# A hybrid attention and RWKV-7 layer: lead-in by halves of the sequence, bias vectors stored from another queue, and priority for the first substitution

## The chip, the cores and the metric

The kernel runs on one core of one Trainium2 chip. The metric is device microseconds of one execution, lower is better. TensorE is called PE (its weight loads PEld), VectorE DVE, ScalarE ACT, GpSimd POOL, and the queue that issues most DMAs SP. ACT issues some DMAs as well.

## What is computed

One decoder layer over 512 tokens and 16 learned meta tokens, with 1024 channels and 16 heads of 64. Attention with a sliding window and RWKV-7 time mixing run side by side on the same projections:

```
h = layer_norm(concat(meta, x), ln0_g, ln0_b)            # 528 x 1024
proj = h @ w_in                                          # q, k, v, RWKV columns, two gates
att = sliding-window attention(q, k, v) with rel_bias[t5_bucket(distance)] and sinks
z = token_shift(RWKV columns, shift_mu)                  # r, k, v, wl, al, gl
decay = exp(-exp(-softplus(-(w0 + tanh(wl) @ w2)) - 0.5)); a = sigmoid(a0 + al @ a2)
S = S * decay + (S @ -kk) (kk a)^T + v k^T ; y = S r     # a recurrence over tokens, per head
rw = (group_norm(y) + bonus) * (sigmoid(gl) @ g2)
merged = sigmoid(gate_att) * att + sigmoid(gate_rwkv) * rw
h = layer_norm(ALPHA * h + merged @ w_out); h = layer_norm(ALPHA * h + relu(h @ w_ff1)**2 @ w_ff2)
```

All arithmetic is float32. A product with a weight matrix is made of three matmuls over rounded high and low parts (hi x hi, hi x lo, lo x hi).

## The kernel before

**Lead-in.** Four tiles xt0 to xt3 of 128 tokens each and the meta tokens xm are loaded and normalised (normalize, L229: statistics on DVE, the inverse root on POOL, the scaling on ACT or DVE). PE then turns each of the eight column tiles (transpose, L303), ACT or DVE scales and shifts it into hfull (L306, L308), ACT rounds it into hhi (L311), and DVE makes the residual hlo (L312). These two, 1024 channels by 528 tokens, are the moving operand of every projection.

**Dense units.** A unit (dense, L366) multiplies one 128-column tile of w_in with all tokens, in two spans of 264 tokens, each 8 x 3 matmuls (L331 to L333) into one of two PSUM banks of the pool dn. After each span evict takes the bank out: ACT scales it (L412), and DVE adds the shifted neighbour (mix, L406). The weights come through load (L263): a DMA into one of two tiles wraw, a rounding on ACT (whi, L258) and a residual on DVE (wlo, L261), with three buffers each. The first units are wa (decay and learning-rate inputs), gl (gate input), k0, r0, ak, v0: the keys, reads and values of the first head pair and the attention keys.

**Scan.** For each of eight head pairs, rwkv_lora (L481) turns wa's rows zw and za into the decay and the rate (tw and ta, L491), rwkv_keys and rwkv_reads build the operands AX and BK, rwkv_scores the score blocks, and rwkv_inverse (L746) inverts 16 x 16 diagonal blocks by substitution: 30 small DVE operations on Xf and ftmp, a copy into Xr, two stores to DRAM. rwkv_inverse_place (L775) loads them back as X and XB, and rwkv_blocks (L791) of the next stage multiplies with X on PE (up, L811).

**Attention bias.** One matmul (tbp, L985) gives the bias by distance for 16 heads, a copy puts it into tbs, and a DMA (L989) stores it 128 times into tbd in DRAM. aside_query loads a slanted view of it (bias, L1056). aside_gate_rwkv loads the gate's matrix gw (L1096) and rounds it on ACT (gwh, L1097).

**What sets the order.** PE's order is written by hand: weave (L379) steps through the dense units and calls other work at the times of a table. The other engines' orders come from a scheduler that takes instructions by priority; the context manager ahead(n) raises it by n. Each engine then runs its own list strictly in that order, and so do the DMA issues of SP and of ACT: an instruction that waits holds all behind it. Buffers go round within a pool by tag, and a tile waits for the readers of the one that had its place.

Of the kernel before, what the change touches and what calls it, by code (L numbers as in the profile page):

```python
# [20 lines left out]
P = 128  # L21
# [110 lines left out]
def hybrid_layer_kernel(ctx: ExitStack, tc: tile.TileContext, I: dict, out: bass.AP):  # L132
# [39 lines left out]
    xt = [xp.tile([P, D], F32, name=f"xt{b}", tag=f"xt{b}") for b in range(4)]  # L172
    xm = xp.tile([NMETA, D], F32, name="xm")
    rows = xp.tile([NCOLS, P], F32, name="rows")
    for b in range(4):
        nc.sync.dma_start(xt[b], I["x"][b * P : (b + 1) * P, :])
    nc.scalar.dma_start(xm, I["meta"])
    nc.scalar.dma_start(rows, I["rows"][0:NCOLS])
    a0, w0 = CONSTS["ident"]
    nc.scalar.dma_start(con[:, a0 : a0 + w0], I["consts"][:, a0 : a0 + w0])  # L180
# [14 lines left out]

    vps = pg.tile([P, 512], F32, name="vps", tag="g")
    pe.transpose(vps[:, :NCOLS], rows, ident[:NCOLS, :NCOLS])
    vc = cst.tile([P, NCOLS], F32, name="vc")
    act.copy(vc, vps[:, :NCOLS])
# [48 lines left out]
    moments0 = [normalize(xt[b], P, str(b), b < 2) for b in range(4)]  # L248
    normalize(xm, NMETA, "m", False)
# [25 lines left out]
    early = {COL_WA: load("w_in", COL_WA // P)}  # L275

    hhi = hpool.tile([P, KT, T], F32R, name="hhi")
    hlo = hpool.tile([P, KT, T], F32R, name="hlo")
    tm = pch.tile([P, 512], F32, name="tm", tag="Y", bufs=PS[3])
    for k in range(KT):  # L280
        pe.transpose(
            tm[:, k * NMETA : (k + 1) * NMETA], xm[:, k * P : (k + 1) * P], ident[:NMETA, :NMETA]
        )
    fm = xp.tile([P, KT, NMETA], F32, name="fm")
    m = slice(0, NMETA)

# [6 lines left out]
    dve.tensor_tensor(fm, fm, cols("ln0_b"), op=ALU.add)
    act.copy(hhi[:, :, m], fm)
    dve.tensor_tensor(hlo[:, :, m], fm, hhi[:, :, m].bitcast(F32), op=ALU.subtract)
    for k in range(KT):
        ks = slice(k * P, (k + 1) * P)
        if k % 2 == 0:
            tp = pg.tile([P, 512], F32, name="tp", tag="g")
        else:  # L300
            tp = pat.tile([P, 512], F32, name="tp", tag="a")
        for b in range(4):
            pe.transpose(tp[:, b * P : (b + 1) * P], xt[b][:, ks], ident)  # L303
        full = xp.tile([P, SEQ], F32, name="hfull", tag="hfull", bufs=4)
        if k % 2 == 0:
            act.activation(full, tp, AF.Identity, bias=vcol("ln0_b", k), scale=vcol("ln0_g", k))  # L306
        else:
            dve.tensor_scalar(  # L308
                full, tp, vcol("ln0_g", k), vcol("ln0_b", k), op0=ALU.mult, op1=ALU.add
            )  # L310
        act.copy(hhi[:, k, NMETA:], full)  # L311
        dve.tensor_tensor(  # L312
            hlo[:, k, NMETA:], full, hhi[:, k, NMETA:].bitcast(F32), op=ALU.subtract
        )

# [83 lines left out]
    def shifted(col, mrow, tag, after, spans=ALLT):  # L399
# [8 lines left out]
        def evict(ps, t0, n):  # L408
            if t0 == spans[0][0]:
                s["z"] = ew.tile([P, T], F32, name=tag, tag=tag)  # L410
                s["edge"] = ew.tile([P, 1], F32, name="edge", tag="edge", bufs=2)
            act.activation(s["z"][:, t0 : t0 + n], ps[:, :n], AF.Copy, scale=dcol("omu", mrow))  # L412
# [336 lines left out]
    def rwkv_inverse(j):  # L749
# [11 lines left out]
        for s in range(B - 1):  # L761
            nj, nt = s + 1, B - 1 - s
            tv = tmp[:, 0 : nj * nt].rearrange("p (j t) -> p j t", j=nj)
            dve.tensor_tensor(  # L764
                tv, Xf[:, 0:nj, s : s + 1].to_broadcast([NB, nj, nt]),
                Nf[:, s : s + 1, s + 1 :].to_broadcast([NB, nj, nt]), op=ALU.mult,
            )
            dve.tensor_tensor(Xf[:, 0:nj, s + 1 :], Xf[:, 0:nj, s + 1 :], tv, op=ALU.add)  # L768
        dve.tensor_copy(Xr, Xf[0:64].rearrange("p a b -> p b a"))
# [219 lines left out]
    nc.sync.dma_start(tbd, tbs.unsqueeze(1).to_broadcast([HEADS, P, P]))  # L989
# [335 lines left out]
    marks = [6]  # L1325
# [91 lines left out]
    with tc.manual_schedule(engines={mybir.EngineType.PE}):  # L1417
        for s in range(-1, PAIRS + 1):
# [257 lines left out]
```

## Time and profile before

| what | us |
|---|---|
| three runs | 995.95, 1003.83, 999.57 |
| their median | 999.57 |
| the profiled execution | 997.59 |
| its span | 995.8 |
| PE busy in the span | 946.2 |
| DVE busy | 654.3 |
| ACT busy | 469.6 |

The profile is of one further execution. Its span is the time from the first to the last instruction; 1.8 us lie around it. A row of the timeline gives the start, the duration, the engine, the line, and the tile written and those read; a bracket gives the engine's idle time just before and what ended it. A busy PE is not PE at its peak: the clock that the throttle granted (PEclk) is listed apart, 1.00 being full.

### The profile page before, as it was taken

Reading aid. Unit: us, or ns where it says so; the run is one execution under the profiler, and the core shown is the slowest. Engines: PE = TensorE matmul, PEld = TensorE weight load, DVE = VectorE, ACT = ScalarE, POOL = GpSimd, SP = SyncE. Lnnn points to the kernel's source line nnn. Section 1 sums busy time; section 2 is a strip of 40 time slices with the busy share of each in tenths; the row PEclk is TensorE's granted clock in tenths of the full one; section 3 lists DMA queues with packets and bytes.
Section 4 is the critical chain, followed back from the end, with each engine's and each line's share of the span. In section 5 each row is a group of like instructions: output and inputs, shape, how many; then the busy total and the mean of one; then the engine's idle time right before and its main releaser. Section 6 shows DMA issues by size and latency. Waiting matters only on the chain.

```text
span 995.8 us, 19206 instructions
## 1 busy us (share of the span) xinstructions
PE 946.2 (95%) x7533; PEld 790.8 (79%) x7533; DVE 654.3 (66%) x1503; ACT 469.6 (47%) x1238; POOL 43.4 (4%) x108
## 2 busy tenths in 40 slices
PE   4999899999999999999998999899999999999996
PEld 3988788888888887878886677788888888888885
DVE  8577688787887878778867865766433234543437
ACT  6535448465584575745736822843422124442220
POOL 2000000010010000100001000100000000000001
PEclk9999899999999999999999999899999999999999
DMA  7544332433224432233444535133232323323232
GB/s 269 94 126 125 99 81 67 126 76 104 76 50 124 104 112 68 70 109 88 129 124 104 171 106 212 64 106 127 86 106 74 117 86 104 95 95 100 71 105 84
DMA packets 82674, 105.47 MB, mean 106 GB/s; under 512 B 47766, under 2 KB 54664, under 8 KB 82584
## 3 DMA queue, kind: packets, MB, share of 16 engines
q1 hardware_dynamic: 81088, 102.16, 35.1%
q10 hardware_dynamic: 1496, 2.08, 0.6%
q8 instruction: 59, 0.97, 0.4%
q14 instruction: 31, 0.25, 0.1%
HBM read 86.29 MB, written 13.74 MB: 100 GB/s over the span
## 4 chain that ended last, share of the span: by engine, by line
PE 69%; DVE 17%; ACT 8%; issue 2%; DMA 2%; SPq 0%; POOL 0%; DVEq 0%; ACTq 0%; POOLq 0%
PE dps L331 12%; PE dps L332 11%; PE dps L333 11%; PE acc L1486 6%; PE acc L1488 6%; PE acc L1487 6%; DVE wlo L261 2%; ACT Z L744 2%; PE sc L659 2%; PE o L1273 2%; PE av L1180 2%; DVE AX L884 2%; PE o L1275 1%; PE o L1274 1%; DVE Xf L768 1%
## 5 line engine op out<-in xcount | busy, mean ns | idle before, releaser
L261 DVE TENSOR_TENSOR wlo<-wraw,whi 128x512 fp32r<-128x512 f32 x242 | 159.4, 685 | 175.3 <-ACT whi L258 174.9
L258 ACT CAST whi<-wraw 128x512 fp32r<-128x512 f32 x242 | 141.8, 618 | 274.3 <-PE dps L332 135.2
L331 PE MATMUL dps<-hhi,whi 128*128 128x264 f32 (+1 forms) x640 | 219.1, 342 | 3.4 <-DVE ftmp L764 1.4
L332 PE MATMUL dps<-hlo,whi 128*128 128x264 f32 (+1 forms) x640 | 204.9, 320 | 1.4 <-DVE hlo L312 1.4
L333 PE MATMUL dps<-hhi,wlo 128*128 128x264 f32 (+1 forms) x640 | 204.1, 319 | 0.4 <-DVE wlo L261 0.4
L331 PEld LDWEIGHTS dps<-hhi,whi 128*128 128x128 f32 x640 | 121.8, 190 | 17.1 <-issue 3.0
L333 PEld LDWEIGHTS dps<-hhi,wlo 128*128 128x128 f32 x640 | 121.4, 190 | 9.1 <-DVE wlo L261 0.6
L332 PEld LDWEIGHTS dps<-hlo,whi 128*128 128x128 f32 x640 | 121.8, 190 | 6.9 <-DVE hlo L312 2.5
L331 PE MATMUL dps<-h1hi,whi 128*128 128x512 f32 (+1 forms) x264 | 100.1, 380 | 3.8 <-ACT h1f L1536 3.8
L332 PE MATMUL dps<-h1lo,whi 128*128 128x512 f32 (+1 forms) x264 | 100.3, 380 | 0.0
L333 PE MATMUL dps<-h1hi,wlo 128*128 128x512 f32 (+1 forms) x264 | 99.9, 379 | 0.0
L331 PEld LDWEIGHTS dps<-h1hi,whi 128*128 128x128 f32 x264 | 50.4, 191 | 12.9 <-ACT h1f L1536 4.1
L332 PEld LDWEIGHTS dps<-h1lo,whi 128*128 128x128 f32 x264 | 50.4, 191 | 9.3 <-DVE h1lo L1542 0.2
L333 PEld LDWEIGHTS dps<-h1hi,wlo 128*128 128x128 f32 x264 | 50.4, 191 | 9.1
L1486 PE MATMUL acc<-whi,hhi 128*128 128x512 f32 x128 | 50.7, 396 | 0.0
L1488 PE MATMUL acc<-whi,hlo 128*128 128x512 f32 x128 | 50.4, 394 | 0.0
L1487 PE MATMUL acc<-wlo,hhi 128*128 128x512 f32 x128 | 50.0, 391 | 0.0
L1486 PE MATMUL acc<-whi,fhi 128*128 128x512 f32 x112 | 43.6, 389 | 0.0
L1487 PE MATMUL acc<-wlo,fhi 128*128 128x512 f32 x112 | 43.6, 389 | 0.0
L1488 PE MATMUL acc<-whi,flo 128*128 128x512 f32 x112 | 43.6, 389 | 0.0
L897 ACT ACTIVATE Z<-ch,PC 64x64 f32<-64x64 f32 x56 | 17.3, 308 | 45.6 <-DVE Z L895 44.3
L744 ACT COPY Z<-vt 64x64 f32<-64x64 f32 x128 | 26.4, 206 | 9.0 <-PE vt L737 7.6
(292 smaller groups left out, 1721.9 us busy)
## 6 DMA issues: line engine op xcount, KB each, us to landing
wraw<-in_w_ff_dram SPq DMA_DIRECT2D x64, 512.0 KB, 3.6
wraw<-in_w_in_dram SPq DMA_DIRECT2D x52, 512.0 KB, 4.1
wraw<-in_w_out_dram SPq DMA_DIRECT2D x8, 512.0 KB, 3.8
xt<-in_x_dram SPq DMA_DIRECT2D x4, 512.0 KB
Nd<-NT SPq DMA_DIRECT2D x16, 128.0 KB, 3.0
bv<-bv SPq DMA_DIRECT2D x8, 256.0 KB
bvm<-bv SPq DMA_DIRECT2D x8, 256.0 KB, 3.4
qs<-qhi SPq DMA_DIRECT2D x16, 128.0 KB, 4.0
```

Source lines behind the costliest of these rows:

```text
L258: act.copy(hi[:n, qs], raw[:n, qs])
L261: dve.tensor_tensor(lo[:n, qs], raw[:n, qs], hi[:n, qs].bitcast(F32), op=ALU.subtract)
L331: pe.matmul(ps, whi, xhi, start=first, stop=False)
L332: pe.matmul(ps, whi, xlo, start=False, stop=False)
L333: pe.matmul(ps, wlo, xhi, start=False, stop=last)
L659: pe.matmul(scs[e][:, c * P : (c + 1) * P], BK[ER[e], 4 * i + c, :], AXg[ER[e], e, 4 * i + c], start=True, stop=True,)
L744: act.copy(Z[2 * i + cc][64 * (1 - e) : 64 * (1 - e) + 64, e, :], vt[64 * cc : 64 * cc + 64, i * P + e * HD : i * P + (e + 1) * HD],)
L884: dve.tensor_tensor(AXg[:, e, cs], AXg[:, e, cs], gqs[e].rearrange("p (c k t) -> p c k t", c=4, k=2), op=ALU.add,)
L1180: pe.matmul(av[64 * e : 64 * e + 64, (2 * i + n) * P : (2 * i + n + 1) * P], vs[:, 2 * i + n], ps[:, 2 * n + e, :], start=(d == 0), stop=( ...
L1486: pe.matmul(acc[b], xhi[k][:, bs], hi[:, ws], start=first, stop=False)
L1487: pe.matmul(acc[b], xhi[k][:, bs], lo[:, ws], start=False, stop=False)
L1488: pe.matmul(acc[b], xlo[k][:, bs], hi[:, ws], start=False, stop=last)
```

## The change

It has three parts.

First, the lead-in. The order of the first loads changes: the identity, blocks 0 and 1 of x, the first weights, blocks 2 and 3; the parameter rows and the meta tokens by ACT's queue. Blocks 2 and 3 use a buffer of AX. Tokens are turned in halves of 256: tokens(0, k) makes four pairs of column tiles of the first half ahead of the first dense unit, and second_tokens(k) the second half, at times 3.6 to 4.2 of the first stage. The generator spans_first runs the first spans of wa, gl and k0 in turn, then their second spans. The low-rank steps move from 9.0 and 10.4 to 16.8 and 17.6.

Second, the bias by distance becomes distance_bias, called at 7.0. Its copy tbs takes the buffer of gw, and the store into tbd is issued by ACT.

Third, the substitution of the first pair gets the priority PRI["up"].

```diff
-    xt = [xp.tile([P, D], F32, name=f"xt{b}", tag=f"xt{b}") for b in range(4)]
+    xt = [xp.tile([P, D], F32, name=f"xt{b}", tag=f"xt{b}") for b in range(2)]
+    xt23 = rw.tile([P, 2, D], F32, name="xt23", tag="AX", bufs=NBUF["AX"])
+    xt += [xt23[:, d] for d in range(2)]
...
+    nc.scalar.dma_start(rows, I["rows"][0:NCOLS])
+    nc.scalar.dma_start(xm, I["meta"])
+    nc.sync.dma_start(con[:, a0 : a0 + w0], I["consts"][:, a0 : a0 + w0])
+    wfirst = wst.tile([P, D], F32, name="wraw", tag="wraw", bufs=WB[2])
     for b in range(4):
+        if b == 2:
+            nc.sync.dma_start(wfirst, I["w_in"][COL_WA // P])
         nc.sync.dma_start(xt[b], I["x"][b * P : (b + 1) * P, :])
...
-    moments0 = [normalize(xt[b], P, str(b), b < 2) for b in range(4)]
-    normalize(xm, NMETA, "m", False)
+    with ahead(500):
+        normalize(xm, NMETA, "m", True)
+        moments0 = [normalize(xt[b], P, str(b), b == 0) for b in range(2)]
...
+    def tokens(u, k):
+        pool_, tag = ((pg, "g"), (pat, "a"))[k // 2 % 2]
+        tp = pool_.tile([P, 512], F32, name="tp", tag=tag)
+        t4 = tp.rearrange("p (d t) -> p d t", d=2)
+        if u == 0:
+            full = xp.tile([P, 2, 2 * P], F32, name="hfull", tag="hfull", bufs=4)
         else:
+            full = rw.tile([P, 2, 2 * P], F32, name="hfull", tag="NT", bufs=NBUF["NT"])
+        for d in range(2):
+            for b in range(2):
+                pe.transpose(
+                    t4[:, d, b * P : (b + 1) * P],
+                    xt[2 * u + b][:, (k + d) * P : (k + d + 1) * P], ident,
+                )
+        for d in range(2):
+            g_, b_ = vcol("ln0_g", k + d), vcol("ln0_b", k + d)
+            if d == 0:
+                act.activation(full[:, d], t4[:, d], AF.Identity, bias=b_, scale=g_)
+            else:
+                dve.tensor_scalar(full[:, d], t4[:, d], g_, b_, op0=ALU.mult, op1=ALU.add)
+        ts_ = slice(NMETA + u * 2 * P, NMETA + (u + 1) * 2 * P)
+        act.copy(hhi[:, k : k + 2, ts_], full)
         dve.tensor_tensor(
+            hlo[:, k : k + 2, ts_], full, hhi[:, k : k + 2, ts_].bitcast(F32), op=ALU.subtract
         )
...
+    with ahead(450):
+        meta_tokens()
+        for k in range(0, KT, 2):
+            tokens(0, k)
+        early = {COL_WA: split(wfirst)}
+    with ahead(450):
+        moments0 += [normalize(xt[b], P, str(b), b == 2) for b in range(2, 4)]
...
-        for s in range(B - 1):
...
+        with ahead(PRI["up"] if j == 0 else 0):
+            for s in range(B - 1):
...
-    tbp = dn.tile([P, 512], F32, name="tbp", tag="dn")
-    pe.matmul(tbp[0:HEADS, 0:P], relb, cv("onehot")[0:NBUCKETS], start=True, stop=True)
-    tbs = at.tile([P, 2 * P], F32, name="tbs", tag="bias", bufs=2)[0:HEADS, 0:P]
-    act.copy(tbs, tbp[0:HEADS, 0:P])
     tbd = dr.tile([HEADS, P, P], F32, name="tbd")
-    nc.sync.dma_start(tbd, tbs.unsqueeze(1).to_broadcast([HEADS, P, P]))
+    def distance_bias():
+        tbp = pat.tile([P, 512], F32, name="tbp", tag="a")
+        pe.matmul(tbp[0:HEADS, 0:P], relb, cv("onehot")[0:NBUCKETS], start=True, stop=True)
+        tbs = at.tile([P, P], F32, name="tbs", tag="gw")[0:HEADS]
+        act.copy(tbs, tbp[0:HEADS, 0:P])
+        nc.scalar.dma_start(tbd, tbs.unsqueeze(1).to_broadcast([HEADS, P, P]))
...
-    unit("wa", COL_WA, shifted(COL_WA, 24, "k", low_rank))
-    unit("gl", COL_GL, shifted(COL_GL, 25, "r", gate_rank))
-    keys(0)
+    def spans_first(first, *then):
+        for gen in (first, *then):
+            for _ in range(KT):
+                yield next(gen)
+        yield from first
+    order += [COL_WA, COL_GL]
+    gl = shifted(COL_GL, 25, "r", gate_rank)
+    k0 = shifted(COL_K, 8, "k", partial(rwkv_keys, 0))
+    units.append(("wa", spans_first(shifted(COL_WA, 24, "v", low_rank), gl, k0)))
+    units.append(("gl", gl))
+    unit("k0", COL_K, k0)
...
-                    (9.0, ("wa",), F(rwkv_lora, 0, 0)),
-                    (10.4, (), F(rwkv_lora, 0, 1)),
-                    (20.0, ("k0",), F(rwkv_sums, 0)),
+                    (16.8, ("wa",), F(rwkv_lora, 0, 0)),
+                    (17.6, (), F(rwkv_lora, 0, 1)),
+                    (24.0, ("k0",), F(rwkv_sums, 0)),
+                    (7.0, (), distance_bias),
+                ] + [(3.6 + 0.2 * k, (), F(second_tokens, k)) for k in range(0, KT, 2)] + [
```

What the change makes of the engines' lists is seen at three places. After the first units' weights the orders of PE, SP, ACT and DVE differ in places up to the end of the first pair's substitution, and from there on in names alone.

On SP, after the constants, before (lw: a low-rank weight, kd: the attention keys):

```order
L427 DMA con<-in_consts_dram 128x1602
L474 DMA lw<-in_lora_dram 128x256
L268 DMA wraw<-in_w_in_dram 128x1024 x2
L1096 DMA gw<-in_gate_w_dram 128x128
L989 DMA tbd<-tbs 2048x1x128
L268 DMA wraw<-in_w_in_dram 128x1024 x2
```

and now, at the same place:

```order
L454 DMA con<-in_consts_dram 128x1602
L501 DMA lw<-in_lora_dram 128x256
L276 DMA wraw<-in_w_in_dram 128x1024 x2
L501 DMA lw<-in_lora_dram 128x256
L1087 DMA bias<-tbd 128x2x128
L1127 DMA gw<-in_gate_w_dram 128x128
L1087 DMA bias<-tbd 128x2x128
L276 DMA wraw<-in_w_in_dram 128x1024
```

The store has left SP, and two loads of its result now stand on both sides of gw's load, ahead of the fourth weight tile of the queue. The first of them waits for the store's end.

On ACT, from the copy of the bias to the low-rank step, before:

```order
L987 COPY tbs<-tbp 16x128
L412 ACTIVATE k<-dps,drv 128x264
L414 COPY edge<-dps 128x1
L1097 CAST gwh<-gw 128x128
L258 CAST whi<-wraw 128x512
L412 ACTIVATE k<-dps,drv 128x264
L258 CAST whi<-wraw 128x512
L438 ACTIVATE twl<-k 64x528
```

and now (v, r, k are the three first units' outputs):

```order
L1019 COPY tbs<-tbp 16x128
L1020 DMA tbd<-tbs 2048x1x128
...
L469 CAST za<-tal 64x528
L1128 CAST gwh<-gw 128x128
L266 CAST whi<-wraw 128x512
L439 ACTIVATE r<-dps,drv 128x264
L266 CAST whi<-wraw 128x512
L474 ACTIVATE sg<-r 128x512
L518 ACTIVATE tw<-dps,drv 128x264 x2
```

The store follows its copy at once, and gwh has moved behind zw and za, but ahead of two weight casts, of gl's second eviction and of the first low-rank evictions tw.

On SP, at the end of the first pair's substitution, before:

```order
L771 DMA xtd_270<-Xf 66x16x16
L1069 DMA qs_1318<-qhi 64x512
L1069 DMA qs_1318<-qlo 64x512
L1069 DMA qs_1319<-qhi 64x512
L1069 DMA qs_1319<-qlo 64x512
L772 DMA Xr_954<-Xr 64x256
L783 DMA XB<-xtd_270 64x8x64 x2
L781 DMA X_1173<-Xr_954 128x8x16
```

and now:

```order
L800 DMA xtd_240<-Xf 66x16x16
L801 DMA Xr_964<-Xr 64x256
L1100 DMA qs_1328<-qhi 64x512
L1100 DMA qs_1329<-qhi 64x512
L1100 DMA qs_1328<-qlo 64x512
L1100 DMA qs_1329<-qlo 64x512
L810 DMA X_1183<-Xr_964 128x8x16
L812 DMA XB<-xtd_240 64x8x64 x2
```

Xr's store has moved ahead of the four stores of the queries, and X's load ahead of XB's but still behind those four.

On DVE, the same end, before:

```order
L764 TENSOR_TENSOR ftmp<-Xf,Nf 66x15
L583 TENSOR_TENSOR AX<-r,Px 64x8x64
L768 TENSOR_TENSOR Xf<-Xf,ftmp 66x15
L583 TENSOR_TENSOR AX<-r,Px 64x8x64
L769 COPY Xr<-Xf 64x256
L1060 SCALAR_TENSOR_TENSOR qlo<-dps,qhi 128x512
```

and now:

```order
L793 TENSOR_TENSOR ftmp<-Xf,Nf 66x15
L568 SCALAR_TENSOR_TENSOR BK<-u,drv,iP 64x8x64
L797 TENSOR_TENSOR Xf<-Xf,ftmp 66x15
L574 SCALAR_TENSOR_TENSOR BKm<-u,drv,iP 64x16
L798 COPY Xr<-Xf 64x256
L568 SCALAR_TENSOR_TENSOR BK<-u,drv,iP 64x8x64
L574 SCALAR_TENSOR_TENSOR BKm<-u,drv,iP 64x16
L610 TENSOR_TENSOR AX<-r,Px 64x8x64
L612 SCALAR_TENSOR_TENSOR rk<-r,vc,kp 128x512
L1091 SCALAR_TENSOR_TENSOR qlo<-dps,qhi 128x512
```

One BK, one BKm and one AX have moved from ahead of Xr's copy to behind it, and rk from behind qlo to ahead of it.

More of the change, by code (lines that the diff above doesn't have):

```diff
@@ L246, in normalize @@
         return mv[:, 0:1], r
[L248 to L249 removed]
+    with ahead(500):
+        normalize(xm, NMETA, "m", True)
+        moments0 = [normalize(xt[b], P, str(b), b == 0) for b in range(2)]
+    vps = pg.tile([P, 512], F32, name="vps", tag="g")
+    pe.transpose(vps[:, :NCOLS], rows, ident[:NCOLS, :NCOLS])
+    vc = cst.tile([P, NCOLS], F32, name="vc")
+    act.copy(vc, vps[:, :NCOLS])
     def split(raw, hi=None, lo=None, n=P):
@@ L293, in hybrid_layer_kernel, with meta_tokens @@
[L293 to L299, printed above, removed]
-        else:
[L301 to L311, printed above, removed]
+    def meta_tokens():
+        tm = pch.tile([P, 512], F32, name="tm", tag="Y", bufs=PS[3])
+        for k in range(KT):
+            pe.transpose(
+                tm[:, k * NMETA : (k + 1) * NMETA], xm[:, k * P : (k + 1) * P], ident[:NMETA, :NMETA]
+            )
+        fm = xp.tile([P, KT, NMETA], F32, name="fm")
+        m = slice(0, NMETA)
+        dve.tensor_tensor(
+            fm, tm[:, 0:P].rearrange("p (k t) -> p k t", k=KT), cols("ln0_g"), op=ALU.mult
+        )
+        dve.tensor_tensor(fm, fm, cols("ln0_b"), op=ALU.add)
+        act.copy(hhi[:, :, m], fm)
+        dve.tensor_tensor(hlo[:, :, m], fm, hhi[:, :, m].bitcast(F32), op=ALU.subtract)
@@ L312, in hybrid_layer_kernel, with second_tokens @@
         dve.tensor_tensor(
-            hlo[:, k, NMETA:], full, hhi[:, k, NMETA:].bitcast(F32), op=ALU.subtract
+            hlo[:, k : k + 2, ts_], full, hhi[:, k : k + 2, ts_].bitcast(F32), op=ALU.subtract
         )
+    def second_tokens(k):
+        with ahead(PRI["dense"]):
+            tokens(1, k)
+    with ahead(450):
[5 more added lines that the diff above has]
+        moments0 += [normalize(xt[b], P, str(b), b == 2) for b in range(2, 4)]
```

42 lines of the change are left out of this document (13 added, 29 removed).

## The prediction

> **What bounds the kernel now.** I read the profile's page first, then TensorE's (PE's) timeline for its waits, then the granted clock by windows. The page's head says that PE is the bound, busy for 95% of the span, with DVE far behind it:
>
> ```profile
> span 995.8 us, 19206 instructions
> PE 946.2 (95%) x7533; PEld 790.8 (79%) x7533; DVE 654.3 (66%) x1503; ACT 469.6 (47%) x1238; POOL 43.4 (4%) x108
> ```
>
> All of the change lies in the first 115 us, so what counts is where PE waits there. Its timeline names the waits in brackets (start, duration, instruction, idle time before it and what ended that):
>
> ```profile
> 26.40 0.39 PE L332 MATMUL dps<-hlo,whi 128*128 128x264 f32 x1
> ...
> 31.04 0.28 PE L332 MATMUL dps<-hlo,whi 128*128 128x264 f32 x1
> 31.16 0.28 PE L333 MATMUL dps<-hhi,wlo 128*128 128x264 f32 x1
> ...
> 36.17 0.36 PE L489 MATMUL dps<-zw,lhi 128*128 128x264 f32 x1 [1.44 <-DVE zw L443]
> ...
> 45.65 0.28 PE L331 MATMUL dps<-hhi,whi 128*128 128x264 f32 x1
> ...
> 59.98 0.39 PE L331 MATMUL dps<-hhi,whi 128*128 128x264 f32 x1 [1.13 <-ACT whi L258]
> ```
> ```profile
> 112.29 1.05 PE L811 MATMUL up<-X,NT 16*32 16x16 f32 x64 [3.71 <-DMA X<-Xr]
> ```
>
> The rows at 31.04 and 31.16 give the undisturbed pace, 0.12 us for a dense matmul over 264 tokens. The last matmul held by the split tokens (hlo) starts at 26.40. PE then waits 1.44 us for the low-rank decay input zw, starts unit r0 at 45.65, and waits 1.13 us for the weights of v0. The largest wait, 3.71 us, is for X, the inverted blocks of the first head pair. What the clock did is in the windows (PE, PEld, DVE, ACT, POOL busy with counts, then PEclk):
>
> ```profile
> 25.00:30.00 5.00, 4.80 (x23) 4.42 (x24) 2.90 (x12) 1.28 (x5) 0.52 (x3) 0.67 0.30 45
> 50.00:85.00 35.00, 32.80 (x273) 31.21 (x272) 26.27 (x60) 15.82 (x40) 0.42 (x4) 1.00 0.55 154
> 85.00:105.00 20.00, 18.14 (x133) 16.12 (x131) 17.72 (x55) 11.13 (x36) 1.56 (x3) 1.00 0.23 65
> 110.00:115.00 5.00, 2.71 (x78) 2.48 (x80) 1.02 (x3) 0.57 (x3) 0.00 (x0) 0.71 0.88 252
> 115.00:120.00 5.00, 5.00 (x82) 3.75 (x79) 2.98 (x6) 0.00 (x0) 0.00 (x0) 0.61 0.01 3
> ```
>
> After the 3.71 us wait the clock stayed at 0.71 and 0.61 of full for ten microseconds, a loss of 5 x 0.29 + 5 x 0.39 = 3.4 us; the ragged start costs 5 x 0.33 = 1.65 us. After the wait of 1.13 us before 59.98 it stayed at 1.00. So the wait for X costs 3.71 + 3.4 = 7.1 us.
>
> **Part 1, the lead-in by halves.** Before, hhi and hlo are made for all 512 tokens of a column tile at once:
>
> ```profile
> 11.34 2.36 ACT L241 ACTIVATE xt<-xt,nm,rs 128x1024 f32<-128x1024 f32 x2
> ...
> 16.91 0.78 ACT L306 ACTIVATE hfull<-tp,vc 128x512 f32<-128x512 f32 x1 [1.15 <-PE tp L303]
> ```
> ```profile
> 14.83 0.81 DVE L243 TENSOR_SCALAR xt<-xt,mv,rs 128x1024 f32<-128x1024 f32 x1
> ...
> 24.46 1.88 DVE L312 TENSOR_TENSOR hlo<-hfull,hhi 128x512 fp32r<-128x512 f32 x3
> ```
> ```profile
> L258 ACT CAST whi<-wraw 128x512 fp32r<-128x512 f32 x242 | 141.8, 618 | 274.3 <-PE dps L332 135.2
> ```
> ```profile
> 85.08 0.87 PE axt L699 x8
> ```
>
> The last block is normalised at 14.83 + 0.81 = 15.64, the first eviction of transposed tokens starts at 16.91, and the last residual ends at 24.46 + 1.88 = 26.34: 9.4 us of ACT and DVE work. Now only two blocks are needed. Blocks 0 and 1 were normalised by 11.34 + 2.36 = 13.7 before; their loads now go ahead of the weights, but the meta tokens go through ACT ahead of block 0, so I keep about 13. With eight of the sixteen transposes (0.11 us each) the first eviction starts near 13.9. Half of 9.4 us is 4.7; ACT's order puts one weight cast (0.62) and the normalisation of block 2 (half of 2.36) between, 1.8 us together. That gives 20.4; I take 21 for the small operations between, with bounds 20 and 22.5. Eight more evictions, each half as wide, add fixed time to both engines, which the end bounds cover.
>
> At 21 PE has done 18 of the 144 dense matmuls of the units wa, gl and k0, and half the transposes. What is left is 126 x 0.12 + 16 x 0.11 + 8 low-rank matmuls x 0.12, with the bias matmul 18.2 us. With three units in turn, the low-rank step stands 14 triples behind the end of wa (14 x 0.36 = 5.0 us), so the 1.44 us wait is covered, and second-half tokens are evicted while PE does the first spans of gl and k0. Unit r0 could start at 39.2, that is 6.4 us earlier than 45.65. Weights are not late: the third split is used six matmuls into the third first span. Moving the parameter rows ahead on ACT's queue and the tokens' tiles into the rings of AX and NT costs nothing that PE sees: those rings are first needed after unit k0.
>
> **Part 2, the vectors by another queue.** These are the bias vectors: a store of 16 x 128 x 128 floats, 1.05 MB in rows of 512 bytes, that ACT now issues. Before, SP issued it behind the load of gw:
>
> ```profile
> 26.47 0.33 SPq L1096 DMA_DIRECT2D gw<-in_gate_w_dram  x1
> 26.85 0.69 SPq L989 DMA_DIRECT2D tbd<-tbs  x1
> ```
> ```profile
> 28.00:40.00 12.00, 10.56 (x78) 10.38 (x78) 5.29 (x10) 7.47 (x17) 0.00 (x0) 0.91 0.74 89
> 40.00:42.00 2.00, 2.00 (x19) 2.00 (x18) 0.78 (x3) 2.00 (x5) 0.00 (x0) 1.00 0.71 269
> ```
> ```profile
> 28.20 0.30 ACT L1097 CAST gwh<-gw 128x128 fp32r<-128x128 f32 x1 [0.70 <-DMA gw<-in_gate_w_dram]
> ...
> 35.20 0.47 ACT L412 ACTIVATE r<-dps,drv 128x264 f32<-128x264 f32 x1
> ...
> 36.69 0.85 ACT L491 ACTIVATE tw<-dps,drv 128x264 f32<-128x264 f32 x2 [0.45 <-PE dps L490]
> ...
> 42.32 0.63 ACT L447 ACTIVATE sg<-r 128x512 f32<-128x512 f32 x1
> ```
>
> From 28 to 40 the DMA engines moved 89 GB/s, 1.07 MB, which is this store; then the rate jumped to 269 GB/s. The store thus takes from 26.85 to 40, 13.1 us, and nobody waited: gw had left before it and was cast at 28.20, 1.73 us after its issue.
>
> In the changed order that cover is gone. The copy tbs takes gw's buffer, and SP's first bias load, which waits for the finished store, stands ahead of the load of gw. On ACT the cast gwh stands ahead of two weight casts, the eviction of gl's second span and the tanh evictions (tw) of the low-rank step. Behind gw thus stand, on SP, the next weight tiles; on ACT, those four; on DVE, gwl with two weight residuals; and PE's low-rank matmuls for za, which need tw's banks. The store is issued after the bias matmul: 39 dense matmuls and 16 transposes after 21, 6.5 us, and one more copy, so about 28.5. It ends at 28.5 + 13.1 = 41.6. One issue (0.4) and gw's 1.73 put gwh at 43.8. Then come 0.30 + 0.62 + 0.47 + 0.62 + 0.63 + 0.43 us of ACT work and 0.5 us for DVE's mix between: tw's first half is free at 47.4, and r0 starts at 48.1 instead of 45.65. So the 6.4 us gained is not only lost, the start is 2.45 us late, after some 8 us in which PE stands. Such a wait lowers the clock; I take the 1.65 us of the ragged start for it, where 3.4 is the other end and nothing the lower one. The wait of 1.13 us before v0 goes, since its split now stands ahead of rk. DVE loses the same time, but from 50 to 85 it has 35 - 26.3 = 8.7 us idle and just catches up at the scores. Sum to there: +2.45 + 1.65 - 1.13 = +3.0 us.
>
> [...]
>
> **Part 3, priority for the first pair's substitution.** Before, the end of the substitution and what follows it stood so on SP, as links of the chain, and on DVE:
>
> ```profile
> 105.37 0.47 SPq L1069 DMA_DIRECT2D qs<-qlo  x1
> ...
> 106.53 0.59 SPq L1069 DMA_DIRECT2D qs<-qlo  x1
> 107.17 0.59 SPq L772 DMA_DIRECT2D Xr<-Xr  x1
> ...
> 109.22 0.62 SPq L781 DMA_DIRECT2D X<-Xr  x1
> ```
> ```profile
> 107.17 2.03 DMA Xr<-Xr
> 109.22 3.02 DMA X<-Xr
> ```
> ```profile
> 101.49 0.75 DVE L541 SCALAR_TENSOR_TENSOR BK<-u,drv,iP 64x512 f32<-64x512 f32 x1
> ...
> 102.48 0.23 DVE L547 SCALAR_TENSOR_TENSOR BKm<-u,drv,iP 64x16 f32<-64x16 f32 x1
> ...
> 103.65 0.69 DVE L583 TENSOR_TENSOR AX<-r,Px 64x512 f32<-64x512 f32 x1
> ...
> 104.37 0.38 DVE L769 COPY Xr<-Xf 64x256 f32<-64x256 f32 x1
> 104.67 0.68 DVE L1060 SCALAR_TENSOR_TENSOR qlo<-dps,qhi 128x512 fp32r<-128x512 f32 x1
> 105.27 0.73 DVE L585 SCALAR_TENSOR_TENSOR rk<-r,vc,kp 128x512 f32<-128x512 f32 x1
> ```
>
> Before, Xr was ready at 104.75, but its store waited behind the four qs stores until 107.17; X was issued at 109.22 when it landed. Now Xr's copy stands ahead of one BK, one BKm and one AX (by starts 0.74, 0.23 and 0.69), so it ends 1.66 us earlier, at 103.1; its store goes at once and lands 2.03 us later, at 105.1. But X now stands behind the qs stores, and these wait for qlo, which stands behind the three and rk: 103.1 + 1.66 + 0.6 + 0.6 = 105.9. Two stores of 0.59 follow, X is issued at 107.1 and lands 3.02 us later at 110.1 instead of 112.29. PE comes there at 108.58 plus the 0.5 that qlo is later, so it idles 1.0 us, too short by the 1.13 us case to lower the clock. Cost after: 1.5 instead of 7.1 us, a gain of 5.6. Bounds: 2.2 if the clock still falls, 7.1 if X is no longer waited for. The matrices XB follow X and are used only after it.
>
> **The sum.** Later orders are the same on all engines but for names. +3.0 - 5.6 = -2.6 us. The profiled execution took 997.59 us (span 995.8), so 995.0; against the runs' median of 999.57 it is 997.0. I say 996.
>
> **Rivals.** A: the store is short or gw arrives before ACT asks for it. For it speaks the rate of 269 GB/s right behind; against it the twelve even microseconds at 89. Moved at 269 GB/s, the store takes 4 us instead of 12, gwh is free before 36, r0 starts at 39.2: -6.4 - 1.13 - 5.6 = -13.1 us, 984.5.
> B, the slower one: PE still idles too long at X and the clock falls. Its place is SP: X behind stores that wait for qlo, on a DVE that is busy for 17.7 of the 20 us from 85 on. It decides when PE's idle time there passes what lies between 1.13 and 3.71 us, so if qlo slips by over 1 us. Price: 1 to 2 us more idle and the 3.4 us again, so the gain of 5.6 becomes about 0 and +3.0 stays: 1000.6. The profile speaks for it by DVE's load, against it by the 2.2 us that X comes earlier.
> C: ACT's hold is much longer than I count, because the store is issued later or runs slower on ACT's queue. With 8 us more there and half the gain at X it is +3.0 + 8 - 2.8 = +8.2 us, 1005.8.
>
> **How the numbers follow.** Forecast 0.62, A 0.15, B 0.18, C 0.05. The likeliest one gives 996, its own range 991 to 1000 (2.5 us for the lead-in, 2 for the clock). The range reaches from A's 984.5 to above B: 985 to 1003. About 1% is what a measurement of this kernel can tell from no change, and is 10 us. Faster by more: A, and a corner of the forecast, 0.17. Slower by more: most of C and a corner of B, 0.08. Within: 0.75.
>
> **What would show it.** Part 1: the first dense matmul before 19, the first spans done by 31, no wait for zw. Part 2: one PE wait of 6 to 10 us ahead of the za matmuls between 39 and 49, ended by ACT's tw, with gwh on ACT waiting for gw's load at about 44 and a low clock behind it. Part 3: Xr's store ahead of the qs stores, PE idle under 1.5 us at the first up matmul, clock 1.00 after it. It is wrong if gwh does not wait, or if the clock falls at X.

## The result, and the profile after

The changed kernel takes 995.84 us (median of 20 executions, 993.76 to 999.78), the kernel before 996.99 us (20, 994.04 to 1003.83). The ratio is 0.999, interval 0.9979 to 1.0: about 1 us less, or nothing. The forecast was 996.0. One execution each of experiments 3 and 6 (1508.4 and 1301.94 us, at a granted clock of 0.56 and 0.66) is left out of their medians and ratios below.

The head of the page after shows that PE is still the bound, and that the profiled span is 2.0 us shorter:

```profile
span 993.8 us, 19221 instructions
PE 944.3 (95%) x7533; PEld 790.9 (80%) x7533; DVE 653.5 (66%) x1507; ACT 471.0 (47%) x1244; POOL 43.1 (4%) x108
```

PE's timeline in the lead-in (start, duration, instruction, then in brackets the idle time before it and what ended that):

```profile
16.09 0.59 PE L358 MATMUL dps<-hhi,whi 128*128 128x264 f32 x1 [0.31 <-ACT hhi L326]
...
48.55 0.59 PE L516 MATMUL dps<-za,lhi 128*128 128x264 f32 x1 [8.90 <-ACT tw L518]
...
49.59 0.42 PE L358 MATMUL dps<-hhi,whi 128*128 128x264 f32 x1
```

The first dense matmul starts at 16.09 instead of 20.30, and the wait of 1.44 us for zw is gone. In its place stands one wait of 8.90 us ahead of the low-rank matmuls for za, and unit r0 starts at 49.59 instead of 45.65. What led to that wait, in the chain of the work that ended last (start, duration, what), and on ACT:

```profile
29.09 13.69 DMA tbd<-tbs
...
42.94 0.38 SPq L1087
...
43.41 1.89 DMA gw<-in_gate_w_dram
...
45.53 0.62 ACT whi L266
...
48.12 0.38 ACT tw L518
```
```profile
45.33 0.30 ACT L1128 CAST gwh<-gw 128x128 fp32r<-128x128 f32 x1 [8.05 <-DMA gw<-in_gate_w_dram]
```

The store lasts 13.69 us. SP's first bias load follows it, gw's load follows that, and gwh on ACT, idle for 8.05 us, follows gw. Behind it come, in order, two weight casts, the eviction of gl and sg on ACT with DVE's residual and mix between, then tw, and PE goes on at 48.55. The windows of the same stretch, and those at X (PE, PEld, DVE, ACT, POOL busy with counts, then PEclk):

```profile
40.00:45.00 5.00, 0.00 (x0) 0.00 (x0) 0.00 (x0) 0.00 (x0) 0.00 (x0) 0.69 0.49 81
45.00:50.00 5.00, 1.46 (x6) 1.46 (x7) 3.13 (x7) 4.21 (x10) 0.00 (x0) 0.50 0.67 198
50.00:55.00 5.00, 5.00 (x36) 5.00 (x34) 3.66 (x8) 3.87 (x11) 0.00 (x0) 0.78 0.45 155
110.00:115.00 5.00, 3.62 (x89) 3.06 (x89) 3.36 (x9) 2.00 (x5) 0.00 (x0) 0.86 0.83 197
115.00:120.00 5.00, 5.00 (x93) 3.50 (x93) 2.46 (x5) 1.43 (x6) 0.00 (x0) 0.80 0.22 84
```

Behind the 8.90 us wait the clock is at half until 52.18. At X, SP and DVE after:

```profile
103.51 0.61 SPq L801 DMA_DIRECT2D Xr<-Xr  x1
106.08 1.12 SPq L1100 DMA_DIRECT2D qs<-qhi  x2
107.31 1.18 SPq L1100 DMA_DIRECT2D qs<-qlo  x2
108.99 0.39 SPq L810 DMA_DIRECT2D X<-Xr  x1
```
```profile
103.11 0.37 DVE L798 COPY Xr<-Xf 64x256 f32<-64x256 f32 x1
...
106.08 0.69 DVE L1091 SCALAR_TENSOR_TENSOR qlo<-dps,qhi 128x512 fp32r<-128x512 f32 x1 [0.27 <-ACT qhi L1090]
```

and PE there:

```profile
111.40 0.73 PE L840 MATMUL up<-X,NT 16*32 16x16 f32 x64 [1.39 <-DMA X<-Xr]
...
113.47 0.69 PE L358 MATMUL dps<-hhi,whi 128*128 128x512 f32 x1
113.96 0.63 PE L359 MATMUL dps<-hlo,whi 128*128 128x512 f32 x1
```

Xr's store now goes at once, X is issued at 108.99, and PE idles 1.39 us instead of 3.71. The clock still falls behind it (0.86 and 0.80 in the two windows), but for 3.4 us where it was 6.8: the dense rows at 113.47 and 113.96 are 0.49 us apart, later 0.43, against 0.23 at full clock (118.94 and 119.17 in the kernel before).

**Where the time went.** In the profiled executions the scores (sc) start at 69.75 instead of 66.67, so the first two parts cost 3.1 us. PE reaches X at 110.01 (111.40 - 1.39) instead of 108.58 (112.29 - 3.71), 1.4 us late: 1.7 us were made up on the way, of which the waits at 73.21, 89.49, 93.14 and 105.40 before (0.58, 1.37, 0.49, 0.40) and at 91.20 and 95.00 now (1.19, 0.64) are 1.0. At X, 2.3 us of idle time go, and 3.2 us less are worked at half clock (6.6 before, from 112.29 to 118.91; 3.4 now), which is worth 1.6 us. 3.1 - 1.7 - 2.3 - 1.6 = -2.5; the two spans differ by -2.0, and the medians of 20 executions by about -1. The 0.7 us of the 1.7 that is in no listed wait stays unassigned.

### The profile page after: what moved, and what is told of

The parts are those of the page before. It is cut to its first block, busy times and chain, and to the rows that moved or that the text cites. A ratio compares the mean times of both kernels' runs of the same rounds, so it can differ in the third digit from the quotient of the medians.

```text
span 993.8 us, 19221 instructions
## 1 busy us (share of the span) xinstructions
PE 944.3 (95%) x7533; PEld 790.9 (80%) x7533; DVE 653.5 (66%) x1507; ACT 471.0 (47%) x1244; POOL 43.1 (4%) x108
## 4 chain that ended last, share of the span: by engine, by line
PE 71%; DVE 14%; ACT 9%; DMA 3%; issue 2%; SPq 0%; POOL 0%; DVEq 0%; ACTq 0%; POOLq 0%
PE dps L358 13%; PE dps L359 11%; PE dps L360 11%; PE acc L1529 6%; PE acc L1531 6%; PE acc L1530 6%; ACT Z L771 2%; PE sc L686 2%; PE o L1304 2%; DVE wlo L269 2%; PE av L1211 2%; DVE AX L913 2%; PE o L1306 1%; DMA tbd<-tbs 1%; DVE ftmp L793 1%
```

## The experiments

All ratios are to the kernel before, with 95% intervals. Each experiment ran beside the kernel before, whose median there was 997.82 us (experiments 1 to 4), 997.97 (5 to 7) and 997.89 (8 to 10), so rows are compared by their ratios, and gains are differences of ratios times these. Starts are those of one profiled execution, in us.

| kernel | median | ratio | r0 | v0 | scores | up, idle before it |
|---|---|---|---|---|---|---|
| before | 996.99 | 1 | 45.65 | 59.98 | 66.67 | 112.29, 3.71 |
| the change | 995.84 | 0.999 (0.9979 to 1.0) | 49.59 | 63.81 | 69.75 | 111.40, 1.39 |
| 1 tbs in its own buffer | 996.75 | 0.9991 (0.9977 to 1.0006) | 41.71 | 63.41 | 69.36 | 110.50, 1.09 |
| 2 without the priority | 1001.13 | 1.0032 (1.0019 to 1.0045) | 49.56 | 64.80 | 70.74 | 113.09, 3.81 |
| 3 the priority alone | 993.9 | 0.9959 (0.9945 to 0.9972) | 45.96 | 60.29 | 66.97 | 110.21, 1.22 |
| 4 X ahead | 994.04 | 0.9962 (0.9948 to 0.9976) | 49.55 | 64.36 | 70.30 | 110.06, none |
| 5 as 1, bias loads by POOL | 990.80 | 0.993 (0.9906 to 0.9953) | 42.86 | 57.22 | 63.16 | 103.88, 1.00 |
| 6 as 1, long rows | 995.84 | 0.9979 (0.9965 to 0.9993) | 41.40 | 62.19 | 68.12 | 109.46, 1.08 |
| 7 priority and X ahead | 992.38 | 0.9943 (0.9925 to 0.996) | 44.37 | 58.71 | 65.40 | 108.88, none |
| 8 store from 128 partitions | 985.94 | 0.9891 (0.9869 to 0.9912) | 41.04 | 54.12 | 60.06 | 100.70, 1.34 |
| 9 as 8, own buffer, X ahead | 983.85 | 0.9864 (0.9842 to 0.9887) | 42.99 | 56.07 | 62.01 | 102.85, none |
| 10 as 5, X ahead | 989.28 | 0.9907 (0.9886 to 0.9928) | 42.68 | 58.71 | 64.64 | 104.41, none |

Starts of one kernel move by about 1 us from one execution to another with the clock (below): experiments 2 and 4 have the same lead-in as the change, and their scores start 1.0 and 0.5 us later.

**1. The copy in its own buffer.** The theory was that gw alone makes PE wait.

```diff
-        tbs = at.tile([P, P], F32, name="tbs", tag="gw")[0:HEADS]
+        tbs = at.tile([P, 2 * P], F32, name="tbs", tag="bias", bufs=2)[0:HEADS, 0:P]
```

> The changed kernel with one edit: the copy tbs takes a buffer of the bias tiles instead of gw's, so that gw's load no longer waits behind the first bias load. Theory 1 (PE's 8.9 us wait for tw comes from gw alone, through SP and ACT): gwh is cast before 31, the wait is gone, and with it the half clock from 48.55 to 52.2, which cost 1.8 us; DVE has 8 us more of room before the scores, enough for its 20.6 us of work there. The scores' sc starts near 59 instead of 69.75, and the kernel takes 10.7 us less, some 1 us of it given back at X: about 986. Theory 2 (another thing holds the same place): the weights of r0 or v0, whose loads still stand on SP behind the bias loads, make PE wait from 44 on, or DVE, busy for 95% of 85 to 105, gives the gain back as a longer wait at X: 990 to 996.

It takes as long as the change. The wait for tw shrinks to 0.84 us, and r0 starts 7.9 us earlier, but PE then stops behind r0, ahead of the first matmul of ak. PE's timeline, SP's and ACT's:

```profile
53.58 0.59 PE L358 MATMUL dps<-hhi,whi 128*128 128x264 f32 x1 [5.86 <-DVE r L433]
```
```profile
43.83 2.06 SPq L1087 DMA_DIRECT2D bias<-tbd  x2
45.93 5.91 SPq L276 DMA_DIRECT2D wraw<-in_w_in_dram  x3
```
```profile
49.53 1.14 ACT L266 CAST whi<-wraw 128x512 fp32r<-128x512 f32 x2 [7.33 <-DMA wraw<-in_w_in_dram]
```

SP issues the bias loads at 43.83, when the store is done, and three weight tiles only behind them. ACT waits 7.33 us for the first of these, v0's. PE needs that tile much later, but r0's eviction on ACT and its mix on DVE stand behind the tile's cast and residual, and for them PE waits 5.86 us. So gw was the first of two holds in a row, both released by the store's end. The first theory falls; its rival, a tile behind the bias loads, is what happened.

**2 and 3. The third part taken away, and alone.**

Experiment 2 edits the changed kernel:

```diff
-        with ahead(PRI["up"] if j == 0 else 0):
+        with ahead(0):
```

and experiment 3 puts the substitution of the kernel before, its 30 operations and the copy into Xr, under the same manager:

```diff
+        with ahead(PRI["up"] if j == 0 else 0):
...
```

> The changed kernel without its third part: the first pair's substitution has its usual priority again. Theory 1 (the third part gains at X, in idle time of PE and in the clock behind it): Xr's store stands behind the four qs stores again, PE waits over 3 us for X, the clock is half for 6 to 7 us instead of 3.4, and the small waits of the copy of v return: 4 to 5 us slower than the changed kernel, about 1000.5. Theory 2 (X stands behind the qs stores with and without the priority, so it matters little): within 1 us of the changed kernel.

> The kernel before with the third part alone: the first pair's substitution gets the priority. Theory 1 (the third part gains 5 us, and the first two lose 3 as measured at the scores): 4 to 5 us faster than the kernel before, about 992.3, and so some 3 us faster than the whole change. Theory 2 (the priority works only together with the later lead-in, which gives DVE time): within 1 us of the kernel before.

Without it the change loses 4.2 us (1.0032 - 0.999, of 997), and alone it gains 4.1 us. The first theory holds in both, and the two figures agree. The profile of experiment 2 has the old order on SP again, and the old wait on PE:

```profile
107.86 0.60 SPq L801 DMA_DIRECT2D Xr<-Xr  x1
...
110.30 0.61 SPq L810 DMA_DIRECT2D X<-Xr  x1
```
```profile
113.09 1.05 PE L840 MATMUL up<-X,NT 16*32 16x16 f32 x64 [3.81 <-DMA X<-Xr]
```

and that of experiment 3 a shorter one, with the old lead-in:

```profile
110.21 0.73 PE L812 MATMUL up<-X,NT 16*32 16x16 f32 x64 [1.22 <-DMA X<-Xr]
```

The first two parts together thus cost 3.2 us (experiment 2 against the kernel before).

**4. X ahead of the last two stores.**

```diff
-        nc.sync.dma_start(X1, blocks(Xrd, 0, [B, P], [8 * B * B, NCH], [1, B]))
+        with ahead(800 if j == 0 else 0):
+            nc.sync.dma_start(X1, blocks(Xrd, 0, [B, P], [8 * B * B, NCH], [1, B]))
```

> The changed kernel with the load of X for the first pair raised in priority, so that on SP it stands ahead of the two qs stores of qlo. Theory 1 (PE's 1.39 us wait is what lets the clock fall at 113.57): X is issued 1.6 us earlier and lands near 109.8, PE does not wait, the clock stays at 1.00, and both the wait and the 1.8 us of half clock are gone: 3.2 us less, about 992.6. Theory 2 (the clock falls because of the small matmuls that follow, up, meta and the scores, whether PE waited or not): only the wait goes, 1.4 us less, about 994.4, with a clock of 0.50 for 3.4 us still there. Theory 3 (the stores of qlo, now behind X, are waited for): no gain.

```profile
107.42 0.53 SPq L811 DMA_DIRECT2D X<-Xr  x1
108.06 1.53 SPq L1101 DMA_DIRECT2D qs<-qlo  x2
```
```profile
110.06 0.85 PE L841 MATMUL up<-X,NT 16*32 16x16 f32 x64
```

X is issued at 107.42, PE does not idle, and the windows from 105 to 125 are at a clock of 1.00. The gain against the change is 2.8 us (0.999 - 0.9962), of 3.2 expected by the first theory; the second would have been 1.4.

**5 and 6. The second hold taken away in two ways.** Both have tbs in a buffer other than gw's. In the first (the upper part of the lines below, on top of experiment 1) POOL issues the first two bias loads; in the second (the lower part) tbs holds each row eight times, so that the store has 256 rows of 4 KB.

```diff
-        nc.sync.dma_start(bias, toe)
+        (nc.gpsimd if j < 2 else nc.sync).dma_start(bias, toe)
...
-        tbs = at.tile([P, P], F32, name="tbs", tag="gw")[0:HEADS]
-        act.copy(tbs, tbp[0:HEADS, 0:P])
-        nc.scalar.dma_start(tbd, tbs.unsqueeze(1).to_broadcast([HEADS, P, P]))
+        tbs = at.tile([P, 4, 2, P], F32, name="tbs", tag="sb", bufs=SBB)
+        tbs = tbs.rearrange("p n e s -> p (n e) s")[0:HEADS]
+        act.copy(tbs, tbp[0:HEADS, 0:P].unsqueeze(1).to_broadcast([HEADS, 8, P]))
+        nc.scalar.dma_start(
+            tbd.rearrange("h (n r) c -> h n (r c)", r=8),
+            tbs.rearrange("h r c -> h (r c)").unsqueeze(1).to_broadcast([HEADS, P // 8, 8 * P]),
+        )
```

> The kernel of the first experiment (tbs in a buffer of its own) with one more edit: POOL issues the first two bias loads, so that on SP no weight tile stands behind them. There PE waited 5.86 us for r0's mix on DVE, which stood behind a residual of weights that SP had loaded 13 us late. Theory 1 (SP's bias loads were the second hold, and nothing stands behind it): that wait and the 2 us of half clock after it go, the scores start near 61 instead of 69.4, the 8 us are kept through X, and the kernel takes 988 to 989. Theory 2 (DVE cannot follow): the scores come 8 us earlier but DVE's list up to the copy into Xr stays 95% busy, PE's idle time before X and before the dense units of the next pair grows, and 4 us or more are given back: 992 to 994. Theory 3 (POOL, waiting for the store's end, holds its clearing of Px, and that the lead-in): 996.

> The changed kernel with a copy tbs that holds each head's row eight times (16 x 1024, in a buffer of its own), so that the same 1.05 MB are stored in 256 rows of 4 KB rather than 2048 of 512 bytes; loads as in the first experiment. Theory 1 (the size of the rows makes the store slow): it runs at over 200 GB/s, lasts 5 us instead of 13, the bias loads leave SP by 37, no weight tile is late, and the kernel takes 988 to 989. Theory 2 (its source on only 16 partitions, or the writing of 1 MB as such, makes it slow): about 89 GB/s and 13 us again, and the kernel takes as long as the first experiment, 996 to 997.

With the loads on POOL the scores start 6.2 us earlier than in experiment 1, the lead is kept through X, and the kernel takes 7.0 us less than before (0.007 x 997.97). That is nearest to the first theory, some 2 us short of it: PE still waits 1.07 us for r0's mix, and in its profile the clock also fell from 22.77 to 26.18. Long rows do nearly nothing; the chain has the store at

```profile
30.01 12.26 DMA tbd<-tbs
```

12.26 us instead of the 13.69 of the change. The size of the rows is not what makes it slow; the second theory holds.

**7. The priority and X ahead on the old lead-in.** The edits of 3 and 4 in the kernel before.

> The kernel before with the third part of the change and X's load raised in priority, without the new lead-in. Theory 1 (the gains at X add up: 4.1 us from the priority, 1.2 us of wait and 1.7 us of half clock from X): 7 us faster than the kernel before, about 991, PE idle under 0.3 us at X and a clock of 1.00 from 105 to 125. Theory 2 (X is no longer what comes last there, the stores of qlo or XB are): 4 to 5 us faster than before, as with the priority alone.

PE does not idle at X and the clock stays at 1.00 there, as the first theory has it. The time lies between the theories, 5.7 us less than before; its interval overlaps that of experiment 3, so the second 1.6 us are not shown.

**8. The store from 128 partitions.** One matmul makes each head's row on eight partitions; tbs again takes gw's buffer, and the bias loads and gw stand on SP as in the change.

```diff
+    rel8 = at.tile([P, 2 * P], F32, name="rel8", tag="bias", bufs=2)
+    pool.tensor_copy(
+        rel8[0:NBUCKETS, 0:P].rearrange("b (h i) -> b h i", i=8),
+        relb.unsqueeze(2).to_broadcast([NBUCKETS, HEADS, 8]),
+    )
...
-        pe.matmul(tbp[0:HEADS, 0:P], relb, cv("onehot")[0:NBUCKETS], start=True, stop=True)
-        tbs = at.tile([P, P], F32, name="tbs", tag="gw")[0:HEADS]
-        act.copy(tbs, tbp[0:HEADS, 0:P])
-        nc.scalar.dma_start(tbd, tbs.unsqueeze(1).to_broadcast([HEADS, P, P]))
+        pe.matmul(tbp[:, 0:P], rel8[0:NBUCKETS, 0:P], cv("onehot")[0:NBUCKETS], start=True, stop=True)
+        tbs = at.tile([P, P], F32, name="tbs", tag="gw")
+        act.copy(tbs, tbp[:, 0:P])
+        nc.scalar.dma_start(
+            tbd.rearrange("h (i r) c -> (h i) r c", i=8), tbs.unsqueeze(1).to_broadcast([P, HEADS, P])
+        )
```

> The changed kernel with the bias by distance made on 128 partitions instead of 16 (each head's row eight times, by a matmul whose weights repeat each head), so that the store of the same 1.05 MB in rows of 512 bytes reads 128 partitions; tbs still takes gw's buffer and the bias loads stay on SP. Theory 1 (16 source partitions make the store slow, since rows eight times as long changed it only from 13.7 to 12.3 us): at 200 GB/s or more it lasts about 5 us, ends near 35, gw is loaded by 38, and neither gw nor a weight tile is late: PE waits under 2 us in all between 38 and 55, and the kernel takes 989 to 991, as with the bias loads on POOL. Theory 2 (writing 1 MB to DRAM takes this long from wherever it comes): 13 us again, the wait of 9 us for tw stays, 996.

ACT issues the store at 28.96, and the bias load that waits for it leaves SP at 34.60, 5.64 us later (13.85 in the change, from 29.09 to 42.94):

```profile
28.96 0.60 ACTq L1026 DMA_DIRECT2D tbd<-tbs  x1
```
```profile
34.60 0.39 SPq L1095 DMA_DIRECT2D bias<-tbd  x1
35.08 0.42 SPq L1135 DMA_DIRECT2D gw<-in_gate_w_dram  x1
```
```profile
40.47 0.36 PE L516 MATMUL dps<-za,lhi 128*128 128x264 f32 x1 [1.00 <-DVE za L470]
...
60.06 1.16 PE L686 MATMUL sc<-AX,BK 64*128 64x128 f32 x16
```
```profile
48.62 0.30 ACT L1136 CAST gwh<-gw 128x128 fp32r<-128x128 f32 x1
```

PE no longer waits for what stands behind gw or behind a weight tile; what is left is 1.00 us for za. The scheduler also put gwh behind tw on ACT in this kernel. That alone is not the gain: experiment 1 had no hold by gw either, and gained nothing while the store was long. At its place in the change, behind za, it would hardly have waited either: gw's load leaves SP at 35.08, and with the 1.89 us that it took in the change gw is in at an estimated 37.0. The scores start at 60.06, 9.7 us earlier than in the change, and the kernel takes 10.9 us less than before. The first theory holds, and the time is 3 us below the lower end of its range.

**9 and 10. The holds together.** Experiment 8 with tbs in a bias buffer and X ahead of the stores of qlo; and experiment 5 with X ahead.

Beside the edit of experiment 4, experiment 9 has this one on top of experiment 8:

```diff
-        tbs = at.tile([P, P], F32, name="tbs", tag="gw")
+        tbs = rel8[:, P : 2 * P]
```

> The kernel with the store from 128 partitions, with tbs in a buffer of the bias tiles instead of gw's, and with X's load ahead of the stores of qlo. Theory 1 (the three holds are separate and their prices add up): 6 us from the lead-in and 2.8 us from X against the changed kernel, 9 us against the kernel before plus what the changed kernel gains: 987 to 988. Theory 2 (once the lead-in is early, DVE's list sets when X is there, so X's place on SP gains nothing): 990 to 991. If the store is still slow, 993.

> The kernel of the experiment with the bias loads issued by POOL, with X's load ahead of the stores of qlo. Theory 1 (prices add up): 1 us of wait at X, and the half clock behind it in the executions in which it falls, go: 2 to 3 us less than with the bias loads on POOL alone, about 988. Theory 2 (DVE's list sets when X is there): as before, 990.8.

In both PE no longer idles at X. By the ratios they are 2.7 and 2.3 us below experiments 8 and 5, but the intervals overlap, so that gain fits the 2.8 us of experiment 4 and isn't shown again. Experiment 9 is 3 us below what its first theory gave, as experiment 8 already was; experiment 10 lies between its two theories (988 and 990.8). What the buffer of its own adds in experiment 9 is not told apart from X. Experiment 9 is the fastest version, 13.6 us (1.4%) below the kernel before, and its interval lies clear of both kernels.

## Why the prediction was right, and where it was off

**Part 1.** The first dense matmul came at 16.09 (before 19 was forecast), and PE was through the three first spans at 30.13 (by 31). With the store out of the way r0 starts at 41.04 (experiment 8), where I had 39.2 as possible: 1.0 of the 1.8 us is a wait for za, which my sum didn't have. "Weights are not late" holds for PE, but v0's tile came late enough to hold ACT and DVE (experiment 1).

**Part 2.** The step was right in place, cause and size: a wait of 8.90 us (6 to 10) ended by tw, gwh at 45.33 (43.8), r0 at 49.59 (48.1), half clock behind it, no wait left before v0. The 1.5 us that r0 is later than forecast come mostly from the store, 13.69 for 13.1 us and issued 0.6 later, and gw, 1.89 for 1.73. The sum to the scores was +3.0; the profile shows +3.1 and experiment 2 +3.2. That agreement is partly luck: r0 came 1.5 us later than forecast, and from r0 to the scores PE took 20.16 us against 21.02 before, 0.9 less, where I had added 0.5 (half clock 1.65, the wait before v0 -1.13). What I had not seen is that the same store holds PE twice. Rival A's second condition, "gw arrives before ACT asks for it", was to bring 984.5; experiment 1 meets it and gains nothing, because v0's weight tile behind the bias loads then holds ACT as gw did.

**Part 3.** This is the term that was mis-sized: 5.6 us forecast, 4.2 and 4.1 measured by taking it away and by having it alone. Two things were off. X landed at 111.4 and not 110.1. I had the two qhi stores gone before qlo was ready at 105.9, but qlo itself had to wait for qhi, which ACT finished only at 106.05 (104.18 before): SP's first qs stores left at 106.08, and X, behind all four, at 108.99 instead of 107.1; its load then took 2.4 us, not 3.0. And "too short by the 1.13 us case to lower the clock" was wrong: it fell after 1.39 us, at a price of 1.7. I had named a fall of the clock at X as a sign of being wrong, and for this part it was. That half of rival B came true; its other half, 1 to 2 us more of idle time, did not. Against this, 1.7 us came back between the scores and X, 1.0 of them in waits that I had left as they were.

**The sum, and luck.** The parts as measured, +3.2 and -4.2, give -1.0 us, and the medians show the same; forecast was -2.6. That the time still came out at 996 is luck of the starting point: the forecast started from 997.59 and 999.57 us, and 20 executions of the kernel before have a median of 996.99. From there -2.6 us would have been 994.4.

**Rival A** has about the right price and the wrong premise: the store isn't short as written. Made short in experiment 8, it gains 10.9 us, against rival A's 13.1. I weighed it by two rates of the trace, 269 GB/s right behind the store and 89 during it, when no run had shown what held the lower one down. The runs narrow it down: rows eight times as long change little (12.26 us instead of 13.69, experiment 6), and from 128 source partitions instead of 16, with the rows also written in another order, the bias load that waits for the store leaves 5.64 us after the store's issue instead of 13.85 (experiment 8).

## What to carry to other kernels

When a wait is taken away, look for what the same event releases next: here one slow store held gw and, behind the same bias loads, a weight tile, and shortening the store freed both. In a queue that issues in order, as SP's did here (in experiment 1 the bias loads at 43.83, when the store was done, and the weight tiles only at 45.93), a load that waits for a late event belongs behind the loads that don't, or on a queue with nothing urgent. A time that comes out as forecast doesn't show that its terms did; here it took experiments of single parts.

## What the runs showed of the hardware

**The store ran at 289 GB/s from 128 source partitions and at 85 from 16.** Windows in the middle of the store, of the change (16 partitions, rows of 512 bytes), of experiment 6 (16, 4 KB) and of experiment 8 (128, 512 bytes); the last three columns are clock, DMA share and GB/s:

```profile
30.00:42.00 12.00, 9.65 (x78) 9.33 (x77) 3.71 (x8) 4.39 (x9) 0.00 (x0) 1.00 0.72 85
```
```profile
31.00:41.00 10.00, 9.15 (x75) 8.92 (x73) 5.89 (x12) 6.90 (x16) 0.00 (x0) 1.00 0.95 106
```
```profile
31.00:33.00 2.00, 2.00 (x19) 2.00 (x18) 0.26 (x1) 0.00 (x0) 0.00 (x0) 1.00 0.99 289
```

85, 106 and 289 GB/s. The second window also has 0.07 MB of SP's queue in its 1.06 MB, so the store alone ran at 99. With eight times as many source partitions the rate was 3.4 times as high (289 against 85), with eight times as long rows 1.2 times (99 against 85). In experiment 8 the rows are also written in another order, which no run tells apart. In all three the DMA engines count as busy for 72% to 99%, and a share of 0.95 went with 106 GB/s where one of 0.99 went with 289.

**The clock changes on a grid of 3.41 us, and one wait's length doesn't decide.** Windows of half a microsecond, of the kernel before and of the change:

```profile
112.00:112.50 0.50, 0.21 (x16) 0.21 (x20) 0.00 (x0) 0.00 (x0) 0.00 (x0) 0.58 0.98 279
118.50:119.00 0.50, 0.50 (x3) 0.39 (x2) 0.44 (x1) 0.00 (x0) 0.00 (x0) 0.59 0.00 0
```
```profile
113.50:114.00 0.50, 0.50 (x4) 0.40 (x3) 0.42 (x1) 0.00 (x0) 0.00 (x0) 0.62 0.86 311
117.00:117.50 0.50, 0.50 (x29) 0.18 (x31) 0.00 (x0) 0.00 (x0) 0.00 (x0) 0.97 0.06 25
```

A window between full and half clock dates the step (0.58 in 112.00 to 112.50: 0.42 us at half, so from 112.08). By that the clock is at half from 26.74 to 30.16 and 112.08 to 118.91 before, from 41.94 to 52.18 and 113.62 to 117.03 after, and from 103.12 to 106.53 in experiment 8: 3.42, 6.83, 10.24, 3.41 and 3.41 us, that is one, two, three, one and one steps. Within one execution the dates lie on one grid: from 26.74 to 112.08 it is 25 steps, from 41.94 to 113.62 it is 21 (85.34 and 71.68 us, 3.41 each).

Three steps of that grid in the kernel before, and one in experiment 4:

```profile
23.33:26.74 3.41, 2.18 (x11) 1.58 (x12) 3.41 (x12) 2.09 (x5) 0.29 (x2) 1.00 0.00 0
71.12:74.53 3.41, 2.71 (x27) 1.90 (x26) 3.38 (x11) 0.56 (x3) 0.20 (x2) 1.00 0.44 90
112.08:115.49 3.41, 3.20 (x84) 2.97 (x84) 0.00 (x0) 0.52 (x2) 0.00 (x0) 0.50 0.81 292
```
```profile
19.32:22.73 3.41, 2.05 (x14) 1.85 (x15) 3.21 (x6) 2.65 (x7) 0.16 (x1) 1.00 0.12 11
```

After the first step, with 11 matmuls and no wait above 0.69 us, the clock fell; after the last, with 14 and waits of 0.79 and 0.75 us, it did not. A wait of 1.39 us at X lowered it, one of 1.37 us between dense units at 89.49 did not. So the length of one wait does not decide; what PE does within a step of the grid fits these cases. At X the clock fell in the five executions in which full-size matmuls filled at most 10% of a step (the kernel before, the change, experiments 2, 3 and 8; in the change 113.47 to 113.62 of 110.20 to 113.62), and not in the other seven, in which they filled at least 27% of every step within 7 us of the first up matmul. What small matmuls count for stays open: in the step from 112.08 they (up, meta and sc, 16 x 16 up to 64 x 128) kept PE busy for 3.20 us and the clock stayed at half until a step mostly full of dense matmuls had passed, while in the step from 71.12, nearly all scm and sc, it stayed full.

The place of a wait on the grid makes one and the same wait cost more or less: behind the 3.8 us for h1f PE works at half clock from 632.28 to 637.73 before and from 630.95 to 634.36 in experiment 3, a loss of 2.7 and of 1.7 us. So medians are compared here, and not single spans.

**A clock that the profile doesn't show.** In the lead-in of the change the dense matmuls start 0.22 us apart, the pace of half clock (in the kernel before, rows at 27.55 and 27.77 in a window at 0.50), and the window has 1.00:

```profile
17.42 0.42 PE L358 MATMUL dps<-hhi,whi 128*128 128x264 f32 x1
17.64 0.42 PE L359 MATMUL dps<-hlo,whi 128*128 128x264 f32 x1
```
```profile
15.00:20.00 5.00, 4.55 (x19) 3.85 (x18) 4.56 (x10) 5.00 (x10) 0.93 (x1) 1.00 0.35 140
```

In experiment 4, with the same lead-in, the rows at 18.73 and 18.86 are 0.13 us apart, so it is not the lead-in that sets the pace. In the change it becomes 0.12 us from 21.46 on, six steps of the grid before 41.94. At the start the pace of the rows is the better clock.
